# Five places of the issue order in an eight-block transformer kernel, and attention copies that VectorE or ScalarE may take

## The chip, the cores and the metric

The kernel runs on one core of a Trainium2 chip. The metric is the device time of one execution in microseconds, the median over runs. PE is TensorE's matmul stream, DVE VectorE, ACT ScalarE, POOL GpSimd, SP the engine that issues the loads.

## The reference

512 tokens of width 1024, fp32, go through four pairs of a mixing layer and a feed-forward layer, each with a residual and an RMS norm ahead of it:

```python
# first_block, layer 0 and 1
sh1, sc1, g1, sh2, sc2, g2 = adaln_params(c, ada_w[layer], ada_b[layer])
h = rms_norm(x, norm_mix_g[layer]) * (1.0 + sc1) + sh1
# layer 0: RG-LRU on half of the channels, stick-breaking attention on the rest
# layer 1: sliding-window attention with sinks
x = x + g1 * mix
h = rms_norm(x, norm_ffn_g[layer]) * (1.0 + sc2) + sh2
x = x + g2 * conv_ffn(h, ...)
# second_block
x = x + diff_attention(rms_norm_2(x, a_norm[0]), ...) @ a_w_o[0]
x = x + squared_relu_mlp(x, m_norm[0], m_w_up[0], m_w_down[0])
k_sh, v_sh = shared_kv(x, kv_norm, kv_w, kv_k_gain, cos, sin)
x = x + dilated_mixer(x, b_norm[0], b_w_q[0], b_q_gain[0], b_w_o[0], k_sh, v_sh, cos, sin)
x = x + squared_relu_mlp(x, m_norm[1], m_w_up[1], m_w_down[1])
```

`dilated_mixer` has three groups of heads: group 0 attends in a window of 128 tokens, groups 1 and 2 with strides of 4 and 16 tokens, and the three outputs are merged by their softmax denominators.

## The kernel before, in words

The residual stream lives on the chip as eight tiles `xs[k]` of 128 channels by 512 tokens. Every matmul operand is split into a high part and a low part (the rest), and each product is three matmuls: high by high, high by low, low by high. So each weight tile passes ACT (cast, the high part) and DVE (`a<-a,a`, the low part), and so does each normalised chunk of x.

A norm ahead of a layer works by halves of 256 tokens (`xnorm`): ACT squares the eight chunks, DVE adds them up, one matmul with a matrix of ones (`b<-t,ones`, called the statistics matmul here) sums over channels, then comes rstd. After that `h_chunk` makes, for each chunk and half, the scaled chunk `t` on DVE, its high part on ACT and its low part on DVE; the layer's first matmuls wait for them. In layer 3 `h_perm` does this with the tokens put in another order.

At the end of a mixing layer `out_quarters` multiplies the attention's output with four quarters of the output weights. The last two quarters go by halves of the tokens (`add_last`), and `residual` adds each result to x, which is what the next norm waits for. With `late` both halves of the third quarter come before the fourth.

All instructions are written by a planner, `Flow` (L83 to L190). Every piece of work is a generator that yields `Op`s with an engine, a cost and a priority; `step` (L130) puts them into the list of their engine, and `dispatch` (L163) takes, whenever the engine is free in the planner's own time, the op with the lowest priority number, and among equals the oldest. The order in which `dispatch` takes them is the program; on the chip each engine then runs its list strictly in that order. Buffers are counted in pools (`a` for operand tiles, `t` for temporaries, `pj`, `ps`, `po`, `pt` for PSUM banks) and a task that finds its pool empty waits.

What the change touches: `layer0_in` (L1090 ff.: six banks are zeroed by fp32 matmuls on a tile that GpSimd clears, L1138, before anything else); `h_chunk` and `h_perm` (priority of the low part, where `P_SECOND` comes after `P_CRIT` as written and `P_LO` before both); `ada_finish` (sums up the modulation of layer 1, one group of four small matmuls `b<-adap,sel` per pair of segments); `four_heads` with its users (`four_heads` runs four heads of one block of 128 queries: scores, mask and maximum, exponentials, in layer 1 a scaling by the denominator, then transposes, copies of the transposed weights out of PSUM, and the product with v), `split`, `fin_qk`, `fin_v`, `sb_job`; and layer 3. There groups 1 and 2 work on a copy of the normalised x with permuted tokens, `x2`, made by `second` after the last unit of group 0 has freed the operand tiles of `x`. The output of layer 3 then has its tokens permuted, and `residual(perm=True)` adds it with a strided access (`x<-x,b`). `join` adds group 0's output and that of groups 1 and 2 together.

Of the kernel before, what the change touches and what calls it, by code (L numbers as in the profile page):

```python
# [10 lines left out]
F32 = mybir.dt.float32  # L11
# [79 lines left out]
class Flow:  # L91
# [35 lines left out]
    def step(s, t, _):  # L127
        while True:
# [22 lines left out]
            for op in r:  # L151
# [4 lines left out]
            for e in sorted({op.eng for op in r}):  # L156
                if not s.busy[e]:
                    s.dispatch(e)
            return

    def dispatch(s, e):
# [7 lines left out]
        op = q.pop(i)[2]  # L169
        cost = op.cost  # L170
# [38 lines left out]
def body(ctx, tc, I, out, upto=8):  # L209
# [133 lines left out]
    one1 = const("one1", (P, 1))  # L343
    adap = const("adap", (P, 192))
# [180 lines left out]

    def proj_tm(u, x, tpair, kinds=()):
# [61 lines left out]
    def h_chunk(x, k, hf, r, g, sh=None):  # L588
# [169 lines left out]
    def ada_finish(l, segs):  # L758
        s0, n = segs[0], 8 * len(segs)
        if l == 0:  # L760
# [4 lines left out]
            return  # L765
        yield ("pt", 1)
# [32 lines left out]
    def fin_qk(ps, tp, dst, isq, gain, rope, dup):  # L799
# [41 lines left out]
        out = acopy if gain is None else (lambda o, a: act(o, a, AF.Identity, scale=gain))  # L841
# [23 lines left out]
    def fin_v(ps, tp, dst):  # L865
        yield acopy(dst.t[:, 2 * tp : 2 * tp + 2, :], ps.rearrange("p (t d) -> p t d", t=2))
# [78 lines left out]
    def split(y, c0, sl, src):  # L945

        hi, lo = y.hi[c0 // 2][:, :, sl], y.lo[c0 // 2][:, :, sl]
        yield acopy(hi, src)
        yield tt(lo, src, hi.bitcast(F32), ALU.subtract)

    def four_heads(mms, mk_, nk, mx, den, negm, pv, oput, r8=None, norm=None):
# [13 lines left out]
        if norm is not None:  # L965
            yield from norm()
            yield [ts(e[i % 2][:, sl(i)], e[i % 2][:, sl(i)], den[:, i : i + 1], None, ALU.mult) for i in (0, 2, 1, 3)]
        w = [tmp(), tmp()]
        for kb in range(nk // P):
# [4 lines left out]
            yield acopy(w[kb], pt) if kb == 0 else vcopy(w[kb], pt, fast=False)  # L974
# [17 lines left out]
    def setup():  # L992
# [6 lines left out]
        yield vcopy(silu32[:, :, 0:1], silu_c.unsqueeze(2))  # L999

# [91 lines left out]
    def layer0_in():  # L1092
# [67 lines left out]
    def layer0(x, pss):  # L1160
# [66 lines left out]
        def sb_job(q, k, v, y, qb, c, done):  # L1227
# [25 lines left out]
            for i in two:  # L1253
# [3 lines left out]
                yield acopy(w[i][:, :nk], pt[:, :nk])  # L1257
# [377 lines left out]
    def h_perm(x, k, order, ready, h0=0, h1=2):  # L1635
# [10 lines left out]
        yield tt(x.l(k)[:, sl], t, x.h(k)[:, sl].bitcast(F32), ALU.subtract, prio=P_SECOND if h0 else P_LO)  # L1646
# [448 lines left out]
```

## Time and profile before

| what | value |
|---|---|
| runs | 2805.18, 2805.64, 2805.73 us, median 2805.64 us |
| the profiled execution's own time | 2801.65 us |
| its span | 2799.9 us, mean granted clock 0.989 |
| busy | PE 98%, DVE 63%, ACT 44%, POOL under 1% |
| chain that ended last | PE 87%, DVE 9%, ACT 2%, DMA 1% |
| loads | 277 MB from HBM, 100 GB/s over the span |

The span is the time between the first and the last instruction that the profile holds; some 1.75 us of the execution lie around it. The profiled execution is 4 us (0.14%) below the median of the runs. A matmul's end is modelled, so a busy PE is not PE at its peak. [...]

### The profile page before, as it was taken

What the parts mean: (1) busy time and instruction counts of PE and PEld (TensorE: products, weight loads), DVE (VectorE), ACT (ScalarE), POOL (GpSimd) and SP (SyncE); (2) the same over time, 40 slices, a digit from 0 to 9 for tenths busy, and PEclk for the clock granted to TensorE, in tenths of its full rate; (3) what the DMA queues carried; (4) which work ended last, traced back from release to release, by engine and by line L of the source; (5) the groups of instructions that cost most, each with busy time, mean ns of one, the idle gap of its engine ahead of it and who ended that gap; (6) DMA issues with size and microseconds to landing.
All of it is one profiled execution on the core that took longest, in us unless ns stands there. A gap on an engine that the chain in (4) does not pass through costs nothing.

```text
span 2799.9 us, 43737 instructions
## 1 busy us (share of the span) xinstructions
PE 2735.3 (98%) x17298; PEld 2381.3 (85%) x17298; DVE 1777.9 (63%) x4114; ACT 1239.8 (44%) x2634; POOL 6.4 (0%) x57
## 2 busy tenths in 40 slices
PE   9999999999989999999999999999999999899999
PEld 7777987889869888899988888889899999788888
DVE  5678986457886444588795333676767767943333
ACT  4684423235744232356553322466656554433221
POOL 0000000000000000000000000000000000000000
PEclk9999999999989999999999999999999999999999
DMA  8335564331112223221222223221112123122331
GB/s 306 103 136 218 190 227 148 103 108 61 62 53 91 90 99 112 91 76 46 84 75 84 98 93 103 99 76 61 65 65 76 60 70 97 63 76 91 105 105 62
DMA packets 80270, 281.90 MB, mean 101 GB/s; under 512 B 8896, under 2 KB 11712, under 8 KB 80064
## 3 DMA queue, kind: packets, MB, share of 16 engines
q1 hardware_dynamic: 80064, 279.10, 29.6%
q8 instruction: 136, 2.23, 0.3%
q14 instruction: 70, 0.57, 0.1%
HBM read 276.97 MB, written 2.10 MB: 100 GB/s over the span
## 4 chain that ended last, share of the span: by engine, by line
PE 87%; DVE 9%; ACT 2%; issue 1%; DMA 1%; SPq 0%; ACTq 0%; DVEq 0%
PE b L304 83%; PE b L310 4%; DVE t L262 2%; DVE t L265 2%; DVE a L262 2%; DVE x L262 1%; DVE x L265 1%; DVE a L265 1%; ACT t L292 1%; DMA a<-in_ada_dram 1%; ACT a L295 0%; ACT L220 0%; DVE t L270 0%; DVE s L262 0%; ACT t L295 0%
## 5 line engine op out<-in xcount | busy, mean ns | idle before, releaser
L304 PE MATMUL b<-a,a 128*128 128x256 f32 (+3 forms) x15024 | 2549.0, 332 | 28.8 <-DVE a L262 14.1
L304 PEld LDWEIGHTS b<-a,a 128*128 128x128 f32 (+1 forms) x15024 | 2199.9, 191 | 316.3 <-issue 38.1
L295 ACT CAST a<-a 128x1024 fp32r<-128x1024 f32 (+2 forms) x354 | 357.0, 1035 | 324.5 <-DVE a L262 199.7
L262 DVE TENSOR_TENSOR a<-a,a 128x1024 fp32r<-128x1024 f32 (+2 forms) x362 | 428.8, 1196 | 28.3 <-ACT a L295 20.1
L292 ACT ACTIVATE t<-b 128x512 f32<-128x512 f32 x150 | 88.9, 598 | 313.7 <-PE b L304 312.6
L262 DVE TENSOR_TENSOR x<-b,x 128x512 f32<-128x512 f32 (+1 forms) x144 | 81.8, 573 | 204.2 <-PE b L304 203.6
L295 ACT COPY t<-b 128x512 f32<-128x512 f32 (+3 forms) x194 | 101.2, 524 | 214.9 <-PE b L304 148.0
L265 DVE SCALAR_TENSOR_TENSOR x<-b,mod,x 128x256 f32<-128x256 f32 (+1 forms) x176 | 104.5, 604 | 114.9 <-PE b L304 114.6
L265 DVE SCALAR_TENSOR_TENSOR a<-a,vec,a 128x256 fp32r<-128x256 f32 x288 | 133.1, 483 | 39.4 <-ACT a L292 38.9
L310 PE MATMUL b<-ident,t 128*128 128x128 f32 x896 | 141.3, 278 | 7.6 <-ACT t L295 2.6
L273 DVE CAST a<-t 128x512 fp32r<-128x512 f32 x64 | 27.4, 428 | 190.4 <-ACT t L292 190.4
L295 ACT COPY a<-b 128x512 f32<-128x512 f32 (+1 forms) x146 | 78.1, 537 | 145.1 <-PE b L304 95.9
L292 ACT ACTIVATE a<-a,vec 128x256 fp32r<-128x256 f32 x288 | 132.1, 501 | 0.6 <-DMA a<-in_kvw_dram 0.4
L310 PEld LDWEIGHTS b<-ident,t 128*128 128x128 f32 x896 | 103.0, 141 | 34.0 <-issue 14.1
L292 ACT ACTIVATE t<-t,s,s 128x256 f32<-128x256 f32 (+3 forms) x192 | 113.4, 593 | 28.4 <-DVE s L265 28.4
L292 ACT ACTIVATE t<-t 128x512 f32<-128x512 f32 x108 | 67.6, 633 | 122.7 <-DVE t L265 121.0
L262 DVE TENSOR_TENSOR t<-t,t 128x256 f32<-128x256 f32 (+5 forms) x201 | 105.3, 530 | 13.8 <-ACT t L292 12.2
L276 DVE TENSOR_REDUCE s<-t 128x8 f32<-128x512 f32 (+1 forms) x84 | 56.7, 675 | 85.5 <-ACT t L292 84.9
L262 DVE TENSOR_TENSOR a<-t,a 128x512 fp32r<-128x512 f32 (+1 forms) x188 | 108.0, 601 | 4.2 <-ACT a L295 1.1
L292 ACT ACTIVATE t<-x 128x256 f32<-128x256 f32 (+1 forms) x120 | 51.5, 431 | 118.5 <-DVE x L265 57.1
L295 ACT CAST a<-t 128x256 fp32r<-128x256 f32 (+1 forms) x124 | 62.6, 510 | 90.4 <-DVE t L262 82.5
L262 DVE TENSOR_TENSOR t<-b,rp 128x256 f32<-128x256 f32 x256 | 94.0, 417 | 0.0
(111 smaller groups left out, 1401.7 us busy)
## 6 DMA issues: line engine op xcount, KB each, us to landing
a<-in_ada_dram SPq DMA_DIRECT2D x96, 512.0 KB, 5.3
a<-in_gu_dram SPq DMA_DIRECT2D x88, 512.0 KB, 4.5
a<-in_mu_dram SPq DMA_DIRECT2D x64, 512.0 KB, 4.1
a<-in_md_dram SPq DMA_DIRECT2D x64, 512.0 KB, 3.8
a<-in_kvw_dram SPq DMA_DIRECT2D x48, 512.0 KB, 3.9
a<-in_dn_dram SPq DMA_DIRECT2D x44, 512.0 KB, 3.8
a<-in_aqkv_dram SPq DMA_DIRECT2D x24, 512.0 KB, 4.0
a<-in_bwq_dram SPq DMA_DIRECT2D x24, 512.0 KB, 4.0
```

The source lines that it names most:

```text
L262: return Op("V", ve(size(o)), lambda: V.tensor_tensor(o, a, b, op), prio=prio)
L265: return Op("V", ve(size(o)) + ptr(sc), lambda: V.scalar_tensor_tensor(o, a, sc, b, op0, op1), prio=prio)
L273: return Op("V", ve(size(o), fast), lambda: V.tensor_copy(o, a))
L276: return Op("V", ve(size(a)), lambda: V.tensor_reduce(o, a, AX.X, ALU.add))
L292: return Op("A", c, lambda: A.activation(o, a, f, scale=scale, **kw), tab=SET_OF.get(f.name), prio=prio)
L295: return Op("A", 0.83e-3 * size(o) + 0.07, lambda: A.copy(o, a), prio=prio)
L304: T.matmul(o, l, r, start=st, stop=sp)
L310: T.transpose(o, a, ident)
```

## The change

An op can now have a twin on another engine: `step` puts both into the lists, and whichever engine comes to it first in the planner's time takes it and strikes the other. This is used for the copies out of PSUM in the attention parts (ACT or DVE) and for the scaling in layer 1 (DVE or ACT). Next to that, five places get another order or another instruction.

```diff
+        twins = [op.twin for op in r if op.twin]
+        for op in r + twins:
...
+        if op.twin:
+            s.pend[op.twin.eng] = [w for w in s.pend[op.twin.eng] if w[2] is not op.twin]
...
+    def either(a, b):
+        a.twin, b.twin = b, a
+        return a
+    def copy(o, a):
+        return either(acopy(o, a), vcopy(o, a, fast=False))
...
+    def zeros(ps, r):
+        return mm(fr(S), (ps, zr, r, True, False))
+    def units_k(x, u, release=False):
...
+        for k in range(8):
+            for tp in range(2):
+                yield x.ready[k][tp]
+                if k == 0:
+                    yield zeros(pss[tp], x.h(0))
...
+            if release and k % 2:
+                put("a", 2)
...
-            yield tt(lo, t, hi.bitcast(F32), ALU.subtract, prio=P_SECOND if hf else P_LO)
+            yield tt(lo, t, hi.bitcast(F32), ALU.subtract, prio=P_LO)
...
+        late = ev()
+        fl.at(fl.now + 15.0, late.set)
+        yield late
...
-            yield [ts(e[i % 2][:, sl(i)], e[i % 2][:, sl(i)], den[:, i : i + 1], None, ALU.mult) for i in (0, 2, 1, 3)]
+            yield [either(ts(e[i % 2][:, sl(i)], e[i % 2][:, sl(i)], den[:, i : i + 1], None, ALU.mult),
+                          act(e[i % 2][:, sl(i)], e[i % 2][:, sl(i)], AF.Identity, scale=den[:, i : i + 1])) for i in (0, 2, 1, 3)]
...
-            yield acopy(w[kb], pt) if kb == 0 else vcopy(w[kb], pt, fast=False)
+            yield copy(w[kb], pt)
...
-        yield ("t", 1)
-        z = tmp()
-        G.memset(z, 0.0)
...
-            yield mm(f4(S), (ps, z[:, :P], z, True, False))
...
+            if k == 0:
+                for ps in pss:
+                    yield zeros(ps, hi[:, :S])
...
-            yield tt(ta.rearrange("p (b r j) -> p b r j", b=4, r=4), o0[:, c].rearrange("p (b r j) -> p b r j", b=4, r=4),
+            yield tt(ta.rearrange("p (b j r) -> p b r j", b=4, r=4), o0[:, c].rearrange("p (b r j) -> p b r j", b=4, r=4),
...
+            if hq < 3:
+                k, q, v = yield from (units(x, *three) if hq == 0 else singly(x, three))
+            else:
+                k, q = yield from singly(x, three[:2])
+                x2_begun = spawn(second(), P_CRIT)
+                v = yield from units_k(x, three[2], True)
...
-        x.free()
...
-        x2_begun = spawn(second(), P_CRIT)
...
-                k = yield from units(x, unit(g, hq, "k"))
+                k = yield from (units_k if g == 1 and hq == 0 else units)(x, unit(g, hq, "k"))
...
-        yield from out_quarters("bwo", ys, made, perm=True)
+        yield from out_quarters("bwo", ys, made)
```

`fin_qk` (where there is no gain), `fin_v`, `split`, the weights' copy in `sb_job` and both `oput` in layer 3 change from `acopy` to `copy` in the same way; the low part in `h_perm` gets `P_LO` too. In all, 54 copies out of PSUM into operand tiles (`a<-b`, 33 of them with 512 columns and 21 with 256) move from ACT to DVE and 25 scalings (17 with 256 columns, 8 with 128) from DVE to ACT; PE loses the 6 fp32 matmuls (12 instructions) and gets 10 single ones of 128x512.

On PE, at the end of layer 1, before. `b_8075` and `b_8093` are transposes of the last attention blocks, `b_8038` and `b_8119` their products with v, `b_8059` the statistics matmul, `b_8021` and `b_8031` matmuls of the output weights:

```order
L304 MATMUL b_8021<-a_7067,a_7572 128x256
L304 MATMUL b_8021<-a_7066,a_7573 128x256
L304 MATMUL b_8038<-t_7944,a_6024 64x256 x2
L304 MATMUL b_8038<-t_7945,a_6024 64x256 x2
L304 MATMUL b_8059<-t_7728,ones 128x256
L310 MATMUL b_8075<-ident,t_7939 128x128 x2
L310 MATMUL b_8075<-ident,t_7940 128x128 x2
L310 MATMUL b_8093<-ident,t_7939 128x128 x2
L310 MATMUL b_8093<-ident,t_7940 128x128 x2
L304 MATMUL b_8119<-t_8073,a_6024 64x256 x2
L304 MATMUL b_8119<-t_8074,a_6024 64x256 x2
L304 MATMUL b_8031<-a_7066,a_7568 128x256
```

The two last blocks of the attention stand behind the statistics matmul, with nothing of the output weights between them. Now, the last attention block (`b_7859` its transposes, a few rows ahead; `b_7876` its product with v):

```order
L316 MATMUL b_7868<-a_6706,a_7459 128x256
L316 MATMUL b_7868<-a_6707,a_7459 128x256
L316 MATMUL b_7868<-a_6706,a_7460 128x256
L316 MATMUL b_7876<-t_7837,a_6022 64x256 x2
L316 MATMUL b_7876<-t_7838,a_6022 64x256 x2
L316 MATMUL b_7878<-a_6706,a_7456 128x256
L316 MATMUL b_7878<-a_6707,a_7456 128x256
```

and, 110 rows further on, the statistics matmul, after which 63 more matmuls of the output weights follow before the first of the feed-forward layer:

```order
L316 MATMUL b_8046<-a_6706,a_7456 128x256
L316 MATMUL b_8046<-a_6707,a_7456 128x256
L316 MATMUL b_8046<-a_6706,a_7457 128x256
L316 MATMUL b_8051<-t_7833,ones 128x256
L316 MATMUL b_8046<-a_6706,a_7459 128x256
L316 MATMUL b_8046<-a_6707,a_7459 128x256
L316 MATMUL b_8046<-a_6706,a_7460 128x256
```

The attention ends ahead of the statistics matmul, which now has the output weights' matmuls on both sides.

On DVE, in layer 3, where `x2` is made (`t<-x,rstd` is the permuted chunk, `a<-t,a` its low part, `rp<-t,row` a rope table), before:

```order
L265 SCALAR_TENSOR_TENSOR a_19335<-a_19333,vec,a_19334 128x256 x2
L262 TENSOR_TENSOR t_19495<-x,rstd 128x4x4x32
L262 TENSOR_TENSOR t_19497<-x,rstd 128x4x4x32
L262 TENSOR_TENSOR t_19498<-x,rstd 128x4x4x32
L262 TENSOR_TENSOR a_19479<-t_19495,a_19478 128x512
L262 TENSOR_TENSOR a_19479<-t_19497,a_19478 128x512
L262 TENSOR_TENSOR a_19481<-t_19498,a_19480 128x512
L262 TENSOR_TENSOR t_19499<-x,rstd 128x4x4x32
L262 TENSOR_TENSOR t_19516<-x,rstd 128x4x4x32
L262 TENSOR_TENSOR rp_19520<-t_19486,row 128x256
L262 TENSOR_TENSOR a_19481<-t_19499,a_19480 128x512
L262 TENSOR_TENSOR a_19483<-t_19516,a_19482 128x512
```

and now, where `t<-b,rp`, `s<-t` and `s_19235` belong to the last q and k units of group 0, whose results PE finishes before the v unit (`b_19229` is the q unit's bank):

```order
L273 TENSOR_SCALAR s_19235<-s_19235 128x8
L266 TENSOR_TENSOR t_19337<-x,rstd 128x4x4x32
L266 TENSOR_TENSOR t_19338<-x,rstd 128x4x4x32
L266 TENSOR_TENSOR t_19339<-x,rstd 128x4x4x32
L266 TENSOR_TENSOR a_19327<-t_19337,a_19326 128x512
L266 TENSOR_TENSOR a_19327<-t_19338,a_19326 128x512
L266 TENSOR_TENSOR a_19329<-t_19339,a_19328 128x512
L266 TENSOR_TENSOR t_19340<-x,rstd 128x4x4x32
L280 TENSOR_REDUCE s_19322<-t_19319 128x8
L266 TENSOR_TENSOR t_19320<-b_19229,rp_14460 128x256
L266 TENSOR_TENSOR a_19329<-t_19340,a_19328 128x512
L266 TENSOR_TENSOR t_19320<-b_19229,rp_14460 128x256
```

The eight chunks now stand among the work of the q unit, that is, before the v unit's results; on PE the 96 matmuls of the v unit, chunk by chunk, come between the q unit and the first matmul on `x2`.

## Rows read from the trace of the kernel before

**Rows 1.** The page of the kernel before, part 1: busy time of each engine.

```profile
PE 2735.3 (98%) x17298; PEld 2381.3 (85%) x17298; DVE 1777.9 (63%) x4114; ACT 1239.8 (44%) x2634; POOL 6.4 (0%) x57
```

**Rows 2.** Waits of PE, whole span: us in total, times, longest us.

```profile
PE b L304 <- DVE a L262: 14.1, 11, 4.7
...
PE b L304 <- ACT a L295: 5.9, 6, 1.3
```

**Rows 3.** Windows: us, busy per engine, then PEclk, DMA share, GB/s.

```profile
20.60:76.80 56.20, 56.20 (x460) 48.32 (x461) 33.86 (x84) 24.69 (x45) 0.20 (x2) 0.95 0.77 286
...
150.00:226.00 76.00, 72.35 (x435) 51.59 (x436) 59.73 (x117) 60.48 (x109) 0.00 (x0) 1.00 0.50 178
...
12.82:26.47 13.65, 11.67 (x68) 6.80 (x64) 11.90 (x40) 6.31 (x11) 0.00 (x0) 0.50 1.03 409
```

**Rows 4.** Groups by line and form, PE, the zeroing matmuls: busy, mean ns.

```profile
L304 PE MATMUL b<-t 128*128 128x512 f32 x12 | 7.7, 812 | 1.3 <-POOL t L1138 1.3
```

**Rows 5.** Timeline of PE: start us, us, instructions [idle before <-releaser].

```profile
279.29 3.93 PE L304 MATMUL b<-a,a 128*128 128x256 f32 x19 [2.77 <-DVE a L262]
...
440.61 1.89 PE L304 MATMUL b<-adap,sel 128*128 128x16 f32 x8 [3.31 <-DVE adap L276]
...
821.54 2.79 PE L310 MATMUL b<-ident,t 128*128 128x128 f32 x8 [1.70 <-DVE t L269]
...
830.00 1.12 PE L304 MATMUL b<-t,a 128*64 128x256 f32 x4 [4.62 <-DVE t L273]
...
1457.48 9.97 PE L304 MATMUL b<-a,a 128*128 128x256 f32 x81 [1.07 <-DVE x L262]
...
2396.50 7.13 PE L304 MATMUL b<-a,a 128*128 128x512 f32 x30
...
2448.24 3.79 PE L304 MATMUL b<-a,a 128*128 128x256 f32 x16 [4.69 <-DVE a L262]
```

**Rows 6.** Windows around five waits, columns as in rows 3.

```profile
439.48:446.31 6.83, 5.70 (x17) 4.84 (x18) 6.45 (x11) 2.67 (x4) 0.10 (x2) 0.50 0.40 144
...
803.90:832.50 28.60, 17.15 (x97) 11.40 (x98) 22.78 (x65) 14.76 (x38) 0.10 (x1) 0.75 0.22 74
...
818.36:835.43 17.07, 9.77 (x35) 6.24 (x36) 11.50 (x31) 6.70 (x18) 0.10 (x1) 0.50 0.44 154
...
2000.00:2013.00 13.00, 7.33 (x32) 4.80 (x31) 12.04 (x22) 7.18 (x15) 0.00 (x0) 0.74 0.24 81
...
2006.20:2016.44 10.24, 7.35 (x28) 5.98 (x28) 10.13 (x29) 4.86 (x12) 0.00 (x0) 0.50 0.00 0
...
2382.00:2450.00 68.00, 57.27 (x428) 51.22 (x429) 61.67 (x138) 31.49 (x79) 0.00 (x0) 0.97 0.19 63
...
2446.52:2453.35 6.83, 5.11 (x22) 4.93 (x23) 3.47 (x6) 0.85 (x2) 0.00 (x0) 0.50 0.21 72
```

**Rows 7.** Groups by form, ACT and DVE: copies of attention.

```profile
L295 ACT COPY a<-b 128x512 f32<-128x512 f32 x114 | 66.5, 585 | 124.5 <-PE b L304 75.3 <-PE b L310 48.8
...
L273 DVE COPY t<-b 128x512 f32<-128x512 f32 x40 | 27.5, 688 | 14.6 <-PE b L310 14.2
```

**Rows 8.** Groups by form, DVE: residuals, normalised chunks and their lo parts.

```profile
L262 DVE TENSOR_TENSOR x<-b,x 128x512 f32<-128x512 f32 x80 | 55.3, 692 | 185.0 <-PE b L304 184.4
...
L262 DVE TENSOR_TENSOR a<-t,a 128x512 fp32r<-128x512 f32 x124 | 85.1, 690 | 4.2 <-ACT a L295 1.1
...
L262 DVE TENSOR_TENSOR x<-b,x 128x256 f32<-128x256 f32 x64 | 26.5, 425 | 19.3 <-PE b L304 19.2
...
L262 DVE TENSOR_TENSOR x<-x,b 128x256 f32<-128x256 f32 x32 | 19.4, 645 | 0.0
...
L262 DVE TENSOR_TENSOR x<-x,b 128x512 f32<-128x512 f32 x16 | 17.4, 1087 | 3.1 <-PE b L304 3.0
...
L262 DVE TENSOR_TENSOR t<-x,rstd 128x512 f32<-128x512 f32 x8 | 8.3, 1077 | 0.0
```

More of the change, by code (lines that the diff above doesn't have):

```diff
@@ L68 @@
 class Op:
-    __slots__ = ("eng", "cost", "fn", "tab", "lat", "task", "prio")
+    __slots__ = ("eng", "cost", "fn", "tab", "lat", "task", "prio", "twin")
     def __init__(s, eng, cost, fn, tab=None, lat=LAT, prio=None):
         s.eng, s.cost, s.fn, s.tab, s.lat, s.prio = eng, cost, fn, tab, lat, prio
+        s.twin = None
 class Event:
@@ L155, in step @@
                 s.pend[op.eng].append((p, s.n, op))
-            for e in sorted({op.eng for op in r}):
+            for e in sorted({op.eng for op in r + twins}):
                 if not s.busy[e]:
@@ L343, in body @@
     one1 = const("one1", (P, 1))
+    zr = const("zr", (P, P), F32R)
     adap = const("adap", (P, 192))
@@ L524, in proj_fm_halves @@
                     then(i, pss[2 * i : 2 * i + 2])
+    def zeros(ps, r):
+        return mm(fr(S), (ps, zr, r, True, False))
+    def units_k(x, u, release=False):
+        yield from u.begin()
+        w = yield from take(u.key)
+        pss = []
+        for tp in range(2):
+            pss.append((yield from getps(*ANY)))
+        for k in range(8):
+            for tp in range(2):
+                yield x.ready[k][tp]
+                if k == 0:
+                    yield zeros(pss[tp], x.h(0))
+                for t in range(2):
+                    o = pss[tp][:, t * 256 : (t + 1) * 256]
+                    tok = slice((2 * tp + t) * P, (2 * tp + t + 1) * P)
+                    hh, hl = x.h(k)[:, tok], x.l(k)[:, tok]
+                    wh, wl = w.w(k, slice(0, 256))
+                    yield mm(3 * fr(256), (o, hh, wh, False, False), (o, hh, wl, False, False), (o, hl, wh, False, k == 7 and t == 1))
+            if release and k % 2:
+                put("a", 2)
+        w.free()
+        for tp in range(2):
+            spawn(u.fin(pss[tp], tp), P_FIN)
+        return u.dst
     def proj_tm(u, x, tpair, kinds=()):
@@ L840, in fin_qk @@
         tk = slice(tp * 256, tp * 256 + 256)
-        out = acopy if gain is None else (lambda o, a: act(o, a, AF.Identity, scale=gain))
+        out = copy if gain is None else (lambda o, a: act(o, a, AF.Identity, scale=gain))
         if not dup:
@@ L865, in fin_v @@
     def fin_v(ps, tp, dst):
-        yield acopy(dst.t[:, 2 * tp : 2 * tp + 2, :], ps.rearrange("p (t d) -> p t d", t=2))
+        yield copy(dst.t[:, 2 * tp : 2 * tp + 2, :], ps.rearrange("p (t d) -> p t d", t=2))
         putps(ps)
@@ L947, in split @@
         hi, lo = y.hi[c0 // 2][:, :, sl], y.lo[c0 // 2][:, :, sl]
-        yield acopy(hi, src)
+        yield copy(hi, src)
         yield tt(lo, src, hi.bitcast(F32), ALU.subtract)
@@ L1256, in sb_job @@
                 yield tr([(pt[:, kb * P : (kb + 1) * P], b[i][:, kb * P : (kb + 1) * P]) for kb in range(qb + 1)])
-                yield acopy(w[i][:, :nk], pt[:, :nk])
+                yield copy(w[i][:, :nk], pt[:, :nk])
                 put("pt")
@@ L1674, in oput @@
             def oput(o):
-                yield acopy(ot[:, :, n * P : (n + 1) * P], o[:, :256].rearrange("p (c t) -> p c t", c=2))
+                yield copy(ot[:, :, n * P : (n + 1) * P], o[:, :256].rearrange("p (c t) -> p c t", c=2))
             yield from four_heads(mms_, mask, nk, mx, den, negm, pv, oput, rs)
@@ L1719, in oput @@
             def oput(o):
-                yield acopy(ot[:, :, n * P : (n + 1) * P], o[:, :256].rearrange("p (c t) -> p c t", c=2))
+                yield copy(ot[:, :, n * P : (n + 1) * P], o[:, :256].rearrange("p (c t) -> p c t", c=2))
             yield from four_heads(mms_, mdil, 256, mx, den, negm, pv, oput, None)
@@ L1808, in layer3 @@
             three = unit(0, hq, "k"), unit(0, hq, "q"), unit(0, hq, "v")
-            k, q, v = yield from (units(x, *three) if hq == 0 else singly(x, three))
+            if hq < 3:
[4 more added lines that the diff above has]
+                v = yield from units_k(x, three[2], True)
             md0, p0 = mk("s", (P, 32), tag="m0"), []
```

10 lines of the change are left out of this document (4 added, 6 removed).

## The prediction

> **What bounds the kernel now.** I read the page's busy times first: PE is busy for 2735.3 us of a span of 2799.9 [rows 1], so some 64 us are all that can be had from waits, and no other engine is near its limit over the whole. A busy PE still loses time where the granted clock is 0.5, so the second thing to look for is stretches at the low level. The table of what PE waited for [rows 2] says who ends the idle time: low parts made by DVE (14.1 us in 11 waits) and high parts made by ACT (5.9 us in 6) lead. The timeline of PE [rows 5] places them: no long wait lies within a layer's bulk, they stand at the seams between layers, and a few in attention tails. The windows [rows 6] then give for each seam the idle time (the window less PE's busy time) and the low-clock stretch that follows it. Half of PE's busy time in such a stretch is counted as loss, because the same work at 1.0 would take half as long. The reader should see that a seam costs twice: the wait itself, and the clock behind it.
>
> So the terms are seam by seam. The price of a matmul at full clock comes from long unbroken runs: 30 of 128x512 in 7.13 us, 0.238 us each, and 81 of 128x256 in 9.97 us, 0.123 us each [rows 5].
>
> **The change, part by part.**
>
> *Start of the program.* The 12 fp32 zeroing instructions go (7.7 us busy, waiting on POOL's clearing first [rows 4]). They ran while the first loads came, so their removal is worth nothing. In their place six 128x512 matmuls stand behind the first chunk's arrival. From 20.60 to 76.80 PE is busy for all of the window's 56.20 us [rows 3], so nothing hides them: 6 x 0.238 = 1.4 us, or 2.9 if all fall in the low-clock stretch, 12.82 to 26.47 at 0.50 [rows 3]. Some of the waits before 20.6 can swallow a part. I take **+2.0**, bounds +1.4 and +2.9.
>
> The clock may add to that. The old kernel kept PE at work from 1.3 us on, and yet the stretch from 12.82 to 26.47 was granted 0.50 [rows 3]; so the early work bought nothing that lasted. [...]
>
> *Four more zeroing matmuls* in layer 3 for the two units that go chunk by chunk: 4 x 0.238 = **+1.0**.
>
> *Layer 0 to its feed-forward (279 us).* PE waits 2.77 us for a low part, and the 19 matmuls behind it take 3.93 us, 0.21 each in place of 0.123 [rows 5]. The low parts of the second half now come right behind their chunks. But fewer matmuls (48, before 66) stand behind the statistics matmul as cover. Bounds: the wait and the 1.6 us of slower matmuls gained, -4.4, or the lost cover, 18 x 0.123 = +2.2. I take **-2.0**.
>
> *The modulation of layer 1 (440 us).* PE stands 3.31 us until DVE has made `adap` [rows 5]. The finishing step now waits 15 us more of the planner's time, and in PE's order the four small matmuls stand 72 matmuls of 128x512 later, 72 x 0.238 = 17 us. DVE's list ahead of that reduction keeps its length, so it is done long before. The wait goes and the low stretch (5.70 us busy at 0.50 [rows 6]) gives back half: 3.31 + 2.85 = **-6.2**; lower bound of the gain 3.3, if the clock falls there anyway. What is late next is the modulated norm of layer 1, some 200 us away.
>
> *Layer 1 to its feed-forward (804 to 835 us).* The window of 28.60 us has 17.15 of PE work, so 11.45 idle, and 9.77 us of work at 0.50 cost 4.9 more [rows 6]: 16.3 us in all. What PE waits for are attention jobs: transposes held by DVE's scaling (1.70) and the product with v held by DVE's copy (4.62 [rows 5]), because DVE does the residuals of the output projection in the same stretch and PE meets the last jobs with no other matmul left in front. The order shown for PE has these jobs ahead of the statistics matmul, with some 110 matmuls (13.5 us) in between, and 63 (7.7 us) behind it. The norm's own chain (statistics, rstd, chunks, low parts) and rope-table work remain on DVE. I keep 6 of the 16.3: **-10**, bounds -4 and -16.
>
> *Layer 2 to its feed-forward (1457 us).* Now the third quarter of the output weights does both halves first, and 33 instead of 66 matmuls cover the chain after the statistics matmul. Worst: 33 x 0.123 = +4.1 of lost cover. Best: 0, if the wait of 1.07 there [rows 5] goes for it. **+2.0**.
>
> *The permuted copy in layer 3 (2000 to 2016 us).* Here PE went one chunk at a time: 13.00 less 7.33, 5.67 idle, and 7.35 at 0.50 cost 3.7 [rows 6]. A chunk costs DVE 1.077 + 0.690 = 1.77 us [rows 8], eight 14.2. It could begin only when the last unit had finished. Now that unit frees two chunks after every 24 matmuls (2.9 us), and its 96 matmuls (11.8 us) run while DVE works; the first unit on the copy then takes the chunks one by one at 12 matmuls (1.5 us) each. The last chunk is wanted 11.8 + 7 x 1.5 = 22 us after the start, DVE needs 14.2 and some 3 for the q unit's rope: 5 us to spare. **-9.4**, lower bound of the gain 5.
>
> *Layer 3 to its feed-forward (2382 to 2453 us).* Idle 68.00 - 57.27 = 10.7, and 5.11 at 0.50 cost 2.6 [rows 6]; the longest wait is 4.69, for a low part [rows 5]. DVE is busy 61.67 of 68. The strided residuals become plain: 32 x (0.645 - 0.425) + 16 x (1.087 - 0.692) = 13.3 us off DVE [rows 8]. The strided write goes to `join`; at the strided price of 0.4 more it is 8 x 0.4 = 3.2, of which two (0.8) fall in the tail. Covered fully, 13.3 would go; the chain behind the statistics matmul cannot, so I take **-10.5**, bounds -6 and -13.
>
> *Low parts' priority at the other seams* changes which of DVE's instructions comes first by a few tenths: 0, bounds -2 and +1.
>
> *Copies and scalings.* 54 copies move to DVE at 0.688 instead of ACT's 0.585 us [rows 7] for 512 columns; 25 scalings go the other way. DVE has room in the stages: in layer 0's attention, 51.59 of 76.00 [rows 3]. PE idles 3.65 us there, and the copies could add or take that: **0**, bounds -3 and +3. [...]
>
> **Sum:** 2.0 + 1.0 - 2.0 - 6.2 - 10 + 2.0 - 9.4 - 10.5 = -33.1 us. Against the profiled execution's 2801.65 that is 2768.5; the median of the runs shown stands 4 us higher, and the time is forecast against it: 2805.64 - 33.1, **2772.5 us**. Every gain here is a gap on PE closed, so no term counts twice.
>
> **The rivals.**
>
> *Seams keep their waits.* If the two seams with most DVE work (layers 1 and 3) keep theirs, since the chain behind the statistics matmul is what really holds them and the moved copies stand in DVE's list ahead of it, 20.5 us of the gain go: -12.6, 2793 us. For it: DVE is busy 22.78 of 28.60 and 61.67 of 68.00 in those windows [rows 6]. Against: in the first, PE waits for attention jobs, not low parts.
>
> *The part does not do what it says.* The planner's costs decide the order; if on the chip the freed buffers come late or `adap` is late again, the waits at 440 and 2000 stay: 33.1 - 15.6 = 17.5, 2788 us. Against: the spare time worked out above is 5 us and more.
>
> *The clock at the start.* Without early work the low level could last for one more stretch like that of 13.65 us [rows 3]: +6.8 us, 2779 us.
>
> *Slower.* DVE works strictly in order. A copy in its list waits for its transposes, and behind it stand masks, maxima and low parts of weights; ACT, which is idle more, no longer takes them out of that queue. If each of the 54 held PE up by its own duration, 54 x 0.688 = 37 us, and the start and layer 2 came out at their upper bounds (+3), the change would come to 37 + 3 - 33 = +7: 2813 us. It decides from about 0.7 us of new PE idle time per moved copy. For it: a wait here costs the clock too. Against: in-stage waits of PE are now a few us in all.
>
> **How the numbers follow.** A measurement of this kernel can tell 0.2%, 5.6 us, from no change. The forecast case (2762 to 2783) has 0.53, a larger gain 0.05, the start's clock 0.05 (within the forecast's own range), the part that does nothing 0.10, seams that keep their waits 0.15; all are faster by over 0.2%, 0.88. Several mishaps that cancel the gain: 0.06. Slower: 0.06. The range runs from 2760 to 2794 and takes in the first two rivals; outside it lie the larger gain, the same and the slower case, some 0.17.
>
> **What would show it.** Right: no wait for `adap`; in layer 3 no chain of waits for ACT's and DVE's chunk parts between the v unit and the permuted k unit; no wait of PE for a copy or scaling at the end of layer 1; fewer stretches at 0.50, the start's aside; strided `x<-x,b` gone and `t<-a,a` of `join` dearer; PE's idle time near 30 us. Wrong: new waits for `a<-b` or `w` copies on DVE within attention, or PE idle time at the two large seams as before.

## The result and the profile after

| | median | runs |
|---|---|---|
| before | 2805.41 us | 2799.47 to 2805.73 (4) |
| changed | 2772.28 us | 2770.68 to 2773.66 (4) |

The ratio is 0.9887, 95% interval 0.9870 to 0.9904: 33.1 us less by the medians, where 33.1 had been forecast, and the range of 2760 to 2794 held it. In the two profiled executions the difference is 31.0 us (2801.65 to 2770.68; spans 2799.9 and 2768.8). That the sum agrees to a tenth is luck: several of its terms were off by 1 to 4 us, and their errors cancelled. The profiles show which.

What PE waited for in the changed kernel (us in total, times, longest):

```profile
PE b L316 <- DVE a L266: 17.2, 9, 4.2
PE b L316 <- DMA a<-in_ada_dram: 11.9, 1, 11.9
...
PE b L316 <- ACT a L299: 2.2, 3, 1.2
```

The waits for ACT's copies (L295 then, 5.9 us [rows 2], L299 now) are down to 2.2 us, and the wait for `adap` is gone. Waits for the low parts that plain subtractions make have grown from 14.1 [rows 2] to 17.2 us; those for operand tiles that DVE makes with a scale or a shift, most of them low parts, (`a` of L265 then, L269 now) fell from 7.6 to 2.8. New are 3.2 us for high parts that ACT makes with a shift (L296). PE's 11.9 us before the first load are idle now; before, it ran the zeroing matmuls there [rows 4] and then still stood 3.20 us for that load.

The page's busy times in the changed kernel:

```profile
PE 2717.3 (98%) x17296; PEld 2373.8 (86%) x17296; DVE 1790.1 (65%) x4155; ACT 1223.5 (44%) x2592; POOL 5.8 (0%) x56
```

Of the span of 2768.8 us PE is idle for 51.5, of 2799.9 it was for 64.6 [rows 1].

The timeline of PE in the changed kernel, at the places of [rows 5] (start us, us, instructions, idle before and what ended it):

```profile
272.08 5.09 PE L316 MATMUL b<-a,a 128*128 128x256 f32 x26 [2.68 <-ACT a L296]
...
452.76 0.96 PE L316 MATMUL b<-adap,sel 128*128 128x16 f32 x8
...
656.93 4.77 PE L316 MATMUL b<-a,a 128*128 128x256 f32 x18 [0.55 <-ACT a L296]
...
824.49 5.11 PE L316 MATMUL b<-a,a 128*128 128x256 f32 x28 [4.21 <-DVE a L266]
...
1433.82 3.35 PE L316 MATMUL b<-a,a 128*128 128x256 f32 x14 [3.50 <-DVE a L266]
...
1443.78 0.38 PE L316 MATMUL b<-a,a 128*128 128x256 f32 x1 [1.16 <-ACT a L299]
...
1986.84 0.40 PE L316 MATMUL b<-a,zr 128*128 128x512 f32 x1
1987.08 3.39 PE L316 MATMUL b<-a,a 128*128 128x256 f32 x27
...
2417.80 2.81 PE L316 MATMUL b<-a,a 128*128 128x256 f32 x16 [3.85 <-DVE a L266]
```

The four small matmuls on `adap` (452.76) stand in an unbroken stream. At 824 and 2417 us one wait of about 4 us is left in each seam. 1433.82 and 1443.78 are new: the seam behind layer 2 got worse. The permuted unit's second zeroing matmul at 1986.84 is followed 0.24 later by matmuls that run through, with no idle time in brackets, where the old kernel stopped for every chunk.

Windows of the changed kernel around the same places (us, busy per engine, then PEclk, which is the granted clock as a share of full speed, DMA share, GB/s):

```profile
790.00:830.00 40.00, 35.78 (x281) 34.78 (x280) 34.49 (x79) 17.59 (x34) 0.20 (x2) 0.96 0.28 93
825.01:828.42 3.41, 3.41 (x18) 3.41 (x18) 2.71 (x4) 0.21 (x1) 0.00 (x0) 0.50 0.00 0
1432.58:1439.41 6.83, 5.59 (x24) 5.42 (x25) 3.88 (x10) 2.14 (x5) 0.00 (x0) 0.50 0.00 0
1985.00:2005.00 20.00, 20.00 (x167) 19.91 (x167) 18.09 (x49) 12.89 (x32) 0.00 (x0) 1.00 0.32 107
2352.00:2421.00 69.00, 64.18 (x483) 57.39 (x481) 56.94 (x149) 35.30 (x91) 0.00 (x0) 0.99 0.23 77
2419.03:2422.45 3.42, 3.42 (x16) 3.24 (x16) 0.95 (x3) 0.89 (x2) 0.00 (x0) 0.50 0.00 0
```

Against [rows 6]: idle time at the end of layer 1 is 4.2 us instead of 11.45 and the low-clock stretch 3.4 us instead of 17.1; the one at 440 and the one at 2006 us are gone; a low stretch of 6.8 us is new at 1432. Behind the start, 20.5 us are granted 0.50 in five stretches, before 47.8 in six.

How long such a stretch lasts isn't fixed by the wait ahead of it. Behind the same 4.2 us wait at the end of layer 1 it is 3.4 us here and in the profiles of e1, e8 and e9, and 6.8 in those of e3 to e7 and e10 to e12 (the labels of the experiments below). Between 224 and 234 us, at the end of layer 0's attention, there is none here and in e8, and one of 3.4 to 6.8 in seven profiles with almost the same waits. So one leg of one profile can be off by some 1.5 us for each stretch that it holds, an estimate: 3.4 us at the loss of 0.44 found below.

How far ahead the changed kernel is at each layer's statistics matmul tells what each seam gave. The rows are from the PE timelines, first before, then after: the first statistics matmul of a seam, and in the last row the second one behind layer 3.

```profile
261.92 0.70 PE L304 MATMUL b<-t,ones 128*128 128x256 f32 x2
...
637.18 0.61 PE L304 MATMUL b<-t,ones 128*128 128x256 f32 x2
...
1192.58 0.61 PE L304 MATMUL b<-t,ones 128*128 128x256 f32 x2
...
1799.92 0.70 PE L304 MATMUL b<-t,ones 128*128 128x256 f32 x2
...
2451.82 1.05 PE L304 MATMUL b<-t,ones 128*128 128x256 f32 x2
```

```profile
263.06 0.59 PE L316 MATMUL b<-t,ones 128*128 128x256 f32 x2
...
630.17 0.61 PE L316 MATMUL b<-t,ones 128*128 128x256 f32 x2
...
1173.04 0.61 PE L316 MATMUL b<-t,ones 128*128 128x256 f32 x2
...
1786.71 0.70 PE L316 MATMUL b<-t,ones 128*128 128x256 f32 x2
...
2420.41 1.05 PE L316 MATMUL b<-t,ones 128*128 128x256 f32 x2
```

The lead is -1.1, 7.0, 19.5, 13.2 and 31.4 us. At the first of them the changed kernel has 18 matmuls (2.2 us) more behind it, so it is in truth 1.1 us ahead. Split by waits and low-clock stretches inside these legs, half of a stretch's busy time counted as loss as in the forecast; a remainder is what the other rows leave of a leg:

| place | forecast | measured |
|---|---|---|
| start and layer 0 | +2.0 and 0 | -1.1 together |
| layer 0 to its feed-forward | -2.0 | +0.2 |
| modulation, 440 us | -6.2 | -6.2 (3.31 and 2.85 gone) |
| into layer 1, second half's low parts | 0 | -1.3 (2.12 to 0.84, in three waits) |
| layer 1 to its feed-forward | -10 | -11.2 (remainder of the leg's -12.5) |
| layer 2 to its feed-forward | +2.0 | +6.3 (lead from 19.5 to 13.2) |
| into layer 3 | 0 | -0.8 (waits 3.53 and 1.83 to 2.79 and 1.78) |
| permuted copy, four zeroing matmuls | -9.4, +1.0 | -8.4 (9.35 gone, 4 x 0.24 came) |
| layer 3 to its feed-forward | -10.5 | -9.0 (remainder of the leg's -18.2) |

### The profile page after: what moved, and what is told of

Its sections match the earlier page's. It is cut to its first block, busy times and chain, and to the rows that moved or that the text cites. A ratio compares the mean times of both kernels' runs of the same rounds, so it can differ in the third digit from the quotient of the medians.

```text
span 2768.8 us, 43736 instructions
## 1 busy us (share of the span) xinstructions
PE 2717.3 (98%) x17296; PEld 2373.8 (86%) x17296; DVE 1790.1 (65%) x4155; ACT 1223.5 (44%) x2592; POOL 5.8 (0%) x56
## 4 chain that ended last, share of the span: by engine, by line
PE 89%; DVE 8%; ACT 1%; issue 1%; DMA 1%; SPq 0%; ACTq 0%; DVEq 0%
PE b L316 85%; PE b L322 4%; DVE t L266 2%; DVE a L266 1%; DVE t L269 1%; DVE a L269 1%; DVE x L269 1%; ACT t L296 0%; DVE x L266 0%; DMA a<-in_ada_dram 0%; DVE s L280 0%; ACT a L299 0%; DMA a<-in_gu_dram 0%; ACT t L299 0%; DVE s L266 0%
## 5 line engine op out<-in xcount | busy, mean ns | idle before, releaser
L316 PE MATMUL b<-a,a 128*128 128x256 f32 (+2 forms) x15024 | 2542.0, 332 | 25.9 <-DVE a L266 17.2
L299 ACT CAST a<-a 128x1024 fp32r<-128x1024 f32 (+2 forms) x354 | 357.4, 1034 | 319.3 <-DVE a L266 199.7
L266 DVE TENSOR_TENSOR x<-b,x 128x512 f32<-128x512 f32 (+1 forms) x192 | 105.7, 557 | 214.4 <-PE b L316 213.5
L296 ACT ACTIVATE t<-b 128x512 f32<-128x512 f32 x150 | 88.9, 598 | 315.0 <-PE b L316 314.3
L299 ACT COPY t<-b 128x512 f32<-128x512 f32 (+3 forms) x183 | 97.0, 534 | 199.4 <-PE b L316 147.2
L269 DVE SCALAR_TENSOR_TENSOR x<-b,mod,x 128x256 f32<-128x256 f32 (+1 forms) x176 | 103.8, 602 | 114.8 <-PE b L316 114.2
L277 DVE CAST a<-t 128x512 fp32r<-128x512 f32 x64 | 27.3, 427 | 190.5 <-ACT t L296 190.5
L269 DVE SCALAR_TENSOR_TENSOR a<-a,vec,a 128x256 fp32r<-128x256 f32 x288 | 132.0, 480 | 19.7 <-ACT a L296 16.3
L296 ACT ACTIVATE a<-a,vec 128x256 fp32r<-128x256 f32 x288 | 131.4, 500 | 0.3 <-DMA a<-in_kvw_dram 0.2
L296 ACT ACTIVATE t<-t,s,s 128x256 f32<-128x256 f32 (+3 forms) x192 | 113.3, 592 | 32.3 <-DVE s L269 32.3
L296 ACT ACTIVATE t<-t 128x512 f32<-128x512 f32 x108 | 67.7, 633 | 133.7 <-DVE t L269 131.9
L299 ACT COPY a<-b 128x512 f32<-128x512 f32 (+1 forms) x104 | 56.9, 547 | 132.3 <-PE b L316 83.9
L299 ACT CAST a<-t 128x256 fp32r<-128x256 f32 (+1 forms) x124 | 62.9, 510 | 93.8 <-DVE t L266 77.5
L296 ACT ACTIVATE t<-x 128x256 f32<-128x256 f32 (+1 forms) x120 | 51.0, 430 | 110.7 <-DVE x L269 50.3
```

What stands on the lines that cost most here:

```text
L266: return Op("V", ve(size(o)), lambda: V.tensor_tensor(o, a, b, op), prio=prio)
L269: return Op("V", ve(size(o)) + ptr(sc), lambda: V.scalar_tensor_tensor(o, a, sc, b, op0, op1), prio=prio)
L277: return Op("V", ve(size(o), fast), lambda: V.tensor_copy(o, a))
L296: return Op("A", c, lambda: A.activation(o, a, f, scale=scale, **kw), tab=SET_OF.get(f.name), prio=prio)
L299: return Op("A", 0.83e-3 * size(o) + 0.07, lambda: A.copy(o, a), prio=prio)
L316: T.matmul(o, l, r, start=st, stop=sp)
```

## The experiments

Each is the changed kernel with one thing undone, unless it says otherwise. Runs of the old kernel beside them had medians of 2801.5 to 2804.1 us; ratios are to those.

**Copies and scalings alone.** The old five places, all twins; the edit is against the old kernel.

```diff
-            yield acopy(w[kb], pt) if kb == 0 else vcopy(w[kb], pt, fast=False)
+            yield copy(w[kb], pt)
...
```

> The old five places with all copies and scalings free to go to VectorE or ScalarE. Theory (each seam has its own cause; the copies and scalings set the order at the end of layers 1 and 2, the five places the waits at 440, 2000 and 2382 us): against the old kernel 11 us less at the end of layer 1, 6 us more at the end of layer 2, little else, so about 2800 us, and the waits near 440, 2000 to 2013 and 2448 us are still there. Rival 1 (the copies are worth nothing alone; the whole gain is the five places): 2805 us, with the waits of the end of layer 1 in place. Rival 2 (dearer copies in VectorE's queue cost time): above 2808 us.

Measured: 2797.52 us, ratio 0.9980 (0.9971 to 0.9989), against the old kernel's 2804.14: 6.6 us less. In the trace the end of layer 1 has the changed kernel's one wait of 4.21 us, the end of layer 2 has its wait:

```profile
1442.41 3.36 PE L316 MATMUL b<-a,a 128*128 128x256 f32 x14 [3.50 <-DVE a L266]
```

and the waits at 440 (3.93), around 2000 and at 2443 us (4.69) are there. Each seam did what the theory says.

**The five places alone**, all copies and scalings on their old engines.

```diff
-            yield copy(w[kb], pt)
+            yield acopy(w[kb], pt) if kb == 0 else vcopy(w[kb], pt, fast=False)
...
```

> The five places as changed, every copy and scaling on its old engine. Theory: the changed kernel's time plus 11 us (end of layer 1 as it was) less 6 us (end of layer 2 as it was) and about 1 us of layer 0: 2776 to 2778 us. Rival 1 (whole gain from the five places): 2772 us. Rival 2 (the copies cost time): 2766 us or less.

Measured: 2779.66 us, ratio 0.9915 (0.9900 to 0.9930). The end of layer 1 is the old one again (1.70 and 4.62 in [rows 5]):

```profile
811.71 0.65 PE L316 MATMUL b<-t,a 128*64 128x256 f32 x4 [1.48 <-DVE t L277]
...
818.17 2.79 PE L322 MATMUL b<-ident,t 128*128 128x128 f32 x8 [1.70 <-DVE t L273]
...
826.62 1.12 PE L316 MATMUL b<-t,a 128*64 128x256 f32 x4 [4.61 <-DVE t L277]
```

So the 11 us at the end of layer 1 belong to the copies and scalings, through the order that the planner then finds, and 24.5 us to the five places. 6.6 and 24.5 add up to 31.1, the whole to 33.1, which differ by less than the runs scatter.

**The copy in `split` back on ACT.**

```diff
-        yield copy(hi, src)
+        yield acopy(hi, src)
```

> The changed kernel, with only the copy in split (the attention output's high part, layers 0 to 2) back on ScalarE. The order of PE at the end of layer 2 is then the old one. Theory (at the end of layer 2 the output's parts stood in VectorE's queue behind residuals and weight parts, and with the late order 33 matmuls less cover the norm): 5 to 6 us less than the changed kernel, 2766 us. Rival (the loss there is the norm's chain, not the copy): 2772 us, with a wait of 3 us near 1434 us.

Measured: 2766.87 us, ratio 0.9872 (0.9858 to 0.9887). At the end of layer 2 only the old 1.07 and 0.50 are left:

```profile
1440.88 9.98 PE L316 MATMUL b<-a,a 128*128 128x256 f32 x81 [1.07 <-DVE x L266]
1451.36 0.70 PE L316 MATMUL b<-t,ones 128*128 128x256 f32 x2 [0.50 <-DVE t L266]
```

That is 5.4 us less than the change by the medians, 4 by the ratios, whose intervals overlap; in the traces the leg from the first statistics matmul ahead of layer 2 to the first ahead of layer 3 is 607.1 us, 613.7 in the changed kernel and 607.3 in the old one. The edit takes twelve copies back to ACT, five of 128x512 at 0.69 us and seven of 128x256 at 0.42, and at this seam it also gives back the old order, which the planner made of it.

**Only layer 1's scalings and `four_heads`' copies free.**

```diff
-        out = copy if gain is None else (lambda o, a: act(o, a, AF.Identity, scale=gain))
+        out = acopy if gain is None else (lambda o, a: act(o, a, AF.Identity, scale=gain))
...
```

> The five places, and of the copies and scalings only two kinds free: the scalings of layer 1 and the copies of the transposed weights in four_heads. Theory: the end of layer 1 keeps its gain (11 us), the end of layer 2 loses nothing, the end of layer 0 has its old 142 matmuls between the two norms: 2764 to 2767 us. Rival (the other copies bring part of the gain, in layers 0 and 3): 2770 us or more.

Measured: 2766.69 us, ratio 0.9872 (0.9856 to 0.9889). These two kinds carry the gain at the end of layer 1; the other copies bring nothing that the medians show, and without them the end of layer 2 has its old waits, 1.07 and 0.50 us.

**Without the 15 us wait.**

```diff
-        late = ev()
-        fl.at(fl.now + 15.0, late.set)
-        yield late
```

> The changed kernel without the 15 us that ada_finish waits. Theory: PE waits again about 3 us for adap near 435 us and the clock falls behind it: 6 us more than the changed kernel, 2778 us. Rival (the wait had only covered something else, so the later place moves a wait to another seam): 2772 us, one wait more and one less.

Measured: 2781.51 us, ratio 0.9919 (0.9904 to 0.9933), 9.2 more than the change; its runs went from 2775 to 2783.

```profile
445.10 1.89 PE L316 MATMUL b<-adap,sel 128*128 128x16 f32 x8 [4.08 <-DVE adap L280]
```

```profile
444.90:451.72 6.82, 6.62 (x20) 5.55 (x21) 5.83 (x10) 2.83 (x6) 0.20 (x2) 0.50 0.28 102
```

The wait is 4.08 and half of 6.62 is 3.3, so 7.4 belong to this place. The two profiled executions differ by more, 12.6 us. Of that, 4.4 stand already at the first statistics matmul behind layer 0's attention (267.46 us, 263.06 in the changed kernel), where the order of PE is still the same: this profile's clock came to stay up later (below) and fell once more at 230 us. What the medians have beyond 7.4 is of the size of this scatter.

**The permuted copy as before.**

```diff
-            if hq < 3:
-                k, q, v = yield from (units(x, *three) if hq == 0 else singly(x, three))
-            else:
...
+            k, q, v = yield from (units(x, *three) if hq == 0 else singly(x, three))
```

> The changed kernel with the permuted copy and the two units by chunks as before (the last unit of group 0 by tokens, x2 begun after it, no zeroing matmuls there). Theory: nine waits of 0.2 to 1.2 us near 1970 to 1982 us, 5.7 us in all, and a stretch of 10 us at clock 0.50: 8.4 us more, 2781 us. Rival (VectorE's 1.77 us per chunk sets the pace in any order, and the changed kernel pays it elsewhere in layer 3): 2774 us or less.

Measured: 2782.02 us, ratio 0.9925 (0.9908 to 0.9941), 9.7 more than the change. The waits are back, eight of 0.15 to 1.24 us as in the old trace, and the low clock with them; the first and the seventh:

```profile
1988.74 0.50 PE L316 MATMUL b<-a,a 128*128 128x256 f32 x2 [0.54 <-ACT a L299]
...
1999.51 0.80 PE L316 MATMUL b<-a,a 128*128 128x256 f32 x2 [1.22 <-ACT a L299]
```

```profile
1988.00:2001.00 13.00, 7.32 (x29) 4.79 (x27) 12.28 (x22) 7.17 (x16) 0.00 (x0) 0.73 0.23 81
1994.02:2004.26 10.24, 7.34 (x28) 6.02 (x27) 10.08 (x29) 4.85 (x13) 0.00 (x0) 0.50 0.00 1
```

Idle 13.00 - 7.32 = 5.7, half of 7.34 is 3.7: the same as in [rows 6]. Together with the 1.0 for zeroing that goes, this is 8.4, and the leg from the first statistics matmul ahead of layer 3 to the second behind it (1788.26 to 2431.99 us) is 10.0 longer than the changed kernel's. The rule leaves something out: between the waits matmuls come by twos and fours, and two of them take 0.50 us (first row), where the long run has 0.123 each.

**The strided access back in the residuals.**

```diff
-        yield from out_quarters("bwo", ys, made)
+        yield from out_quarters("bwo", ys, made, perm=True)
...
```

> The changed kernel with the strided access back in the residuals of layer 3 and a plain write in join. Theory (13.3 us of VectorE's time stands on PE's path at this seam): waits between 2375 and 2430 us as in the old kernel, 9.8 us more, 2782 us. Rival (the norm's chain behind the statistics matmul sets the end there, VectorE's earlier work is covered): 2775 us or less.

Measured: 2781.13 us, ratio 0.9921 (0.9906 to 0.9935), 8.9 more. The waits of the old seam return, five of them, from 0.70 to 4.70; two are:

```profile
2384.47 0.66 PE L322 MATMUL b<-ident,t 128*128 128x128 f32 x4 [1.93 <-ACT t L299]
...
2428.02 3.78 PE L316 MATMUL b<-a,a 128*128 128x256 f32 x16 [4.70 <-DVE a L266]
```

DVE's forms in the changed kernel show what was traded (busy, mean ns):

```profile
L266 DVE TENSOR_TENSOR x<-b,x 128x512 f32<-128x512 f32 x96 | 66.3, 691 | 191.2 <-PE b L316 190.6
...
L266 DVE TENSOR_TENSOR x<-b,x 128x256 f32<-128x256 f32 x96 | 39.4, 423 | 23.2 <-PE b L316 23.0
...
L266 DVE TENSOR_TENSOR t<-a,a 128x512 f32<-128x512 f32 x8 | 8.7, 1111 | 0.0
```

All residuals of these forms now cost 691 and 423 ns; `join` (`t<-a,a`) costs 1111, and stood at 694 before:

```profile
L262 DVE TENSOR_TENSOR t<-a,a 128x512 f32<-128x512 f32 x8 | 5.4, 694 | 0.0
```

That is 13.3 us off at the seam and 8 x 0.42 = 3.3 on, mostly elsewhere. `join` now writes with a step of four fp32 elements: 1111 ns in this trace, against 694 without.

**The old priority of the low parts.**

```diff
-            yield tt(lo, t, hi.bitcast(F32), ALU.subtract, prio=P_LO)
+            yield tt(lo, t, hi.bitcast(F32), ALU.subtract, prio=P_SECOND if hf else P_LO)
...
```

> The changed kernel with the old priority for the second half's low parts in h_chunk and h_perm (order of VectorE only). Theory: a few tenths at each of eight seams: 2772 to 2775 us, the second wait behind the statistics matmul at the seam into layer 1 back from 0.6 to 2 us. Rival (the early low parts are what took the wait and the low clock from the seams at 280 and 657 us): 2778 us or more.

Measured: 2771.91 us, ratio 0.9887 (0.9873 to 0.9902), the change's own time. The wait at the seam into layer 1 is 2.12 again instead of 0.55; the medians do not show it.

**The old zeroing**, in the kernel of e4_norm_and_w.

```diff
+        z = tmp()
+        G.memset(z, 0.0)
...
-                    yield zeros(ps, hi[:, :S])
```

> The kernel of e4_norm_and_w with the old zeroing: GpSimd clears a tile and six fp32 matmuls zero the banks from 1.3 us on, no zeroing matmuls behind the first chunk. Theory (the new zeroing matmuls stand on PE's path at the start, 1.4 to 2.9 us, and early work changes nothing that lasts): 2 us less than that kernel, 2765 us. Rival (without early work the clock stays low longer in some executions: the last rise at the start lay between 24 and 35 us in the changed kernel and its variants, at 26 and 28 us in two profiles with early work): 5 us less in the mean and a narrower spread of the runs. Second rival: no difference, within 1 us.

Measured: 2766.76 us, ratio 0.9872 (0.9858 to 0.9887), against 2766.69: the second rival, no difference. The early zeroing matmuls brought no calmer clock here: this profile has 0.50 again from 22.16 to 32.40 us.

```profile
22.16:32.40 10.24, 9.81 (x50) 8.02 (x51) 5.03 (x14) 2.96 (x6) 0.00 (x0) 0.50 1.03 405
```

**The zeroing threefold**, in the same kernel; the 12 more add nothing.

```diff
+                for ps in pss + pss:
+                    yield mm(fr_(S), (ps, zr, hi[:, :S], False, False))
```

> The kernel of e4_norm_and_w with the six zeroing matmuls at the start three times over (12 more, which add nothing). Theory (they are on PE's path): 12 x 0.238 = 2.9 us more at full clock, 5.7 us at the low one: 2770 to 2773 us. Rival (PE waits there for loads and the modulation's chain anyway, so they are hidden): 2767 to 2768 us.

Measured: 2771.56 us, ratio 0.9890 (0.9875 to 0.9904): 4.9 more than 2766.69, 0.41 us each. By the medians they are on PE's path, at a price between that of 1.00 and that of 0.50, though the intervals of the two ratios overlap. For the six of the change this gives 2.4 us as an estimate, but e9, which has none of them there, is not faster. Its profile shows a part of the reason: behind the first load PE waits 3.4 us for DVE and ACT until 25 us, where e4's waits 2.0. The rest is within the scatter of the start (below), so what the six cost is not settled.

**`split`'s low part first.**

```diff
-        yield tt(lo, src, hi.bitcast(F32), ALU.subtract)
+        yield tt(lo, src, hi.bitcast(F32), ALU.subtract, prio=P_LO)
```

> The changed kernel with the low part in split given the priority that goes first (P_LO); its copy stays free to go to VectorE. The planner then orders the end of layer 2 anew, too: the norm's statistics stand 35 matmuls behind the last transposes and two products more. Theory (the loss at the end of layer 2 comes from the output's low part waiting in VectorE's queue): the wait of 3.5 us near 1434 us goes, 3 to 6 us less, 2767 to 2770 us. Rival (the late order itself, with little cover, costs it): 2772 us.

Measured: 2777.40 us, ratio 0.9914 (0.9898 to 0.9931): 5.1 us more than the change, a miss for both. The planner now put the last scaling of the attention's output (DVE, L269) behind the norm's chunks and two weight parts, and PE stands for it:

```profile
1440.78 0.48 PE L322 MATMUL b<-ident,a 128*128 128x128 f32 x1 [8.65 <-DVE a L269]
```

The run tells nothing of the low part; it shows that a priority moves the whole seam.

**The late order off.**

```diff
-        late = wide and not x3.ready[k3][0].done
+        late = False
```

> The changed kernel with add_last never taking the late order, all copies as changed. At the end of layer 2 the fourth quarter's first half then stands ahead of the third quarter's second half, and about 64 matmuls stand behind the statistics matmul again. Theory (the loss there is the copy on VectorE and the low part behind it, which come late; the late order only answers to that): PE meets the fourth quarter about 30 matmuls earlier and waits there longer than 3.5 us; no gain, 2772 to 2776 us. Rival (the late order with its little cover is the loss): 2766 us.

Measured: 2766.26 us, ratio 0.9876 (0.9857 to 0.9894), 6.0 less than the change. The theory as written falls: the wait does not grow, 1.37 and 0.45 us remain.

```profile
1438.64 9.94 PE L316 MATMUL b<-a,a 128*128 128x256 f32 x81 [1.37 <-DVE x L266]
```

In this order the planner also gave the last copy of `split` to ACT, as it did in the old kernel. So the loss at the end of layer 2 is the late order together with the copy on DVE that goes with it; the late order with the copy on ACT was not run, and which of the two weighs more stays open.

Four of these kernels (e3, e4, e9, e12), at 2766.3 to 2766.9 us, beat both the old and the changed one: ratios of 0.9872 to 0.9876 to the old one, and some 5.5 us under the change. They cannot be told apart.

## Why the prediction was right, and where it was not

*Time and sign*: right, and by the mechanism forecast: gaps on PE at the seams, each with its low-clock stretch behind it. Undoing one part brought its seam back and left the waits of the others as they were (e5, e6, e7); so the terms did add. The tenth of a microsecond is luck, as the terms below show.

*Half of a low-clock stretch* was a little too much. The forecast's own rows have 0.21 us for a matmul in place of 0.123; in the trace of the changed kernel one of 128x256 starts 0.213 us after the one before it at 0.50, and 0.120 at 1.00 (medians). So such a stretch costs 0.44 of its busy time, some 0.2 us less than forecast for each of the shorter ones.

*PE's idle time* came to 51.5 us, 39.6 without the wait for the first load, where the forecast's sign was near 30. All of the sum taken off 64.6 gives 31.5; but a part of the sum is clock and not idle time, and 7.7 us of zeroing work turned into idle time. By the totals, waits of about 64.6 - 51.5 + 7.7 = 20.8 us were closed and the clock gave some 0.44 x 27.3 = 12.0, an estimate; the ten new zeroing matmuls take 2.4 of that back at 0.238 each.

*Modulation* (-6.2), *permuted copy* (-8.4 with its zeroing): the waits and low stretches forecast went; undone, the first cost 7.4 us by the trace and 9.2 by the medians, the second 10.0 and 9.7. The spare time of 5 us was enough: no wait is left there.

*End of layer 1* (-10): -11.2. The sign "no wait of PE for a copy or scaling at the end of layer 1" came true; what is left, 4.21 us, is a weight's low part.

*End of layer 3* (-10.5): -9.0 as the remainder (7.4 if the permuted copy gave 10.0), 8.9 by e7. The term was sized on DVE's 13.3 us, less a guess for the norm's chain; the wait of 3.85 that stays is again a weight's low part, behind DVE's second-half norm.

*End of layer 2* (+2.0, bounds 0 and +4.1): the one step that failed outright. It measured +6.3, above its upper bound. The bound counted only the cover behind the statistics matmul (33 matmuls), and of that 1.16 + 0.31 us came. It left out the seam's other wait, ahead of the statistics matmul: PE now reached the fourth quarter when its low part stood behind two weight parts and residuals in DVE's list:

```profile
1428.14 0.68 DVE L277 CAST a<-b 128x512 fp32r<-128x512 f32 x1
...
1433.08 0.69 DVE L266 TENSOR_TENSOR a<-b,a 128x512 fp32r<-128x512 f32 x1
```

The copy ends at 1428.8, the low part starts at 1433.1, and PE has waited 3.50 us. And it left out the clock: 5.59 us of work at 0.50 cost 2.8. Together 3.50 + 1.16 + 0.31 + 2.8, less the 1.07 [rows 5] and 0.51 of before, is 6.2.

*Layer 0 to its feed-forward* (-2.0): +0.2; the wait only moved from a low part to a high part (2.77 to 2.68). *Start and layer 0*: +2.0 forecast, -1.1 measured in all. How much of this is the start and how much the copies in layer 0 (0 forecast, bounds of 3) is not settled. With the old copies there (e4) the first statistics matmul comes at 264.14, and the change reaches it at 263.06 with 2.2 us more work done: 3.3 us for the copies, which would leave +2.2 for the start. But seven other kernels whose order of PE is the change's own up to there reach it between 261.55 and 267.46. In the waits of that stage the copies gained about 1.3 us (5.3 in e4, 4.0 in the change). One reading behind the term was wrong, too: the 51.59 us of 76.00 in layer 0's attention [rows 3] are the weight loads' (PEld); DVE was busy for 59.73.

*The rivals.* Seams that keep their waits, and the part that does nothing: no; e5 to e7 bring back, each for its part, waits that the changed kernel does not have. Slower through DVE's queue: of that kind only the end of layer 2 was found, 5 to 6 us and not 37, and there the late order has its share. The clock at the start: it does come, in some executions, at a few us.

## What to carry to other kernels

Where one engine is busy for 98% of the span, list its gaps, add to each nearly half (0.44 here) of the work in the low-clock stretch behind it, and ask of every change which of these seams it touches; such terms add up. Letting a planner choose the engine of a copy moves more than the copy: it shifts what the planner believes to be ready, and with it the order at the next seam, for better (end of layer 1) or worse (end of layer 2), so look at each seam's order after such a change. When a bound is made for a lost cover, count the wait ahead of it and the clock as well.

## What was not expected of the hardware

At the start the granted clock is not the same from one profile to the next, although the order of PE's first 1800 instructions is the same in the changed kernel, e5_no_15us, e8_old_lo_prio and five more (e3, e6, e7, e11, e12). In e8_old_lo_prio the clock first rose at 24.18 us and stayed up. Its timeline of PE (the zeroing matmuls, the four behind them that wait for ACT, and the long run):

```profile
21.96 2.43 PE L316 MATMUL b<-a,zr 128*128 128x512 f32 x5
24.77 0.60 PE L316 MATMUL b<-one,t 128*128 128x1 f32 x4 [0.37 <-ACT t L299]
...
28.53 9.60 PE L316 MATMUL b<-a,a 128*128 128x256 f32 x78
```

In e5_no_15us it rose at 18.23 already, so that the same five zeroing matmuls were through after 1.43 us in place of 2.43. But PE then waited 2.60 us for ACT, whose part comes at about 24.8 us in either case, the clock fell, and the work that PE sets the pace of ran at 0.50:

```profile
20.89 1.43 PE L316 MATMUL b<-a,zr 128*128 128x512 f32 x5
24.92 0.92 PE L316 MATMUL b<-one,t 128*128 128x1 f32 x4 [2.60 <-ACT t L299]
...
31.70 10.46 PE L316 MATMUL b<-a,a 128*128 128x256 f32 x72
```

```profile
25.06:35.30 10.24, 10.24 (x54) 8.65 (x55) 4.97 (x14) 2.54 (x4) 0.00 (x0) 0.50 1.02 404
```

So an early rise cost time: the long run begins at 31.70 in place of 28.53. In the changed kernel the clock fell at 26.29 and rose last at 29.70 us, and its long run begins at 30.04. The other profiles of this order agree. Where the clock first rose between 24.0 and 24.5 us (e6, e8, e12), it stayed up, and PE starts its 401st instruction at 61.5 to 62.0 us; where it first rose between 16.1 and 18.4 us (the other five), it fell again, and that instruction starts at 63.0 to 66.2. This is up to 4.8 us between executions of one order, a good part of their scatter, and a reason not to compare single profiled times. Early zeroing matmuls did not remove it: in e9_old_zeroing the last rise came at 32.40 us.
